# Chunk scores of an RWKV-7 scan as four 64x64 products, their masks for two heads at a time

## The chip, the cores and the metric

The kernel runs on one core of one Trainium2 chip. The metric is the device time of one launch in microseconds, the median of three runs. The engines are TensorE (PE; its weight loads are a row of their own, PEld), VectorE (DVE), ScalarE (ACT), GpSimd (POOL) and SyncE (SP, which starts most DMAs).

## What is computed

The reference is one inference step of a four-layer backbone: layers 0 and 3 are long convolutions, layer 1 is latent attention, and layer 2 is a bidirectional RWKV-7 mixer over 1024 latent and 128 context tokens with 16 heads of 64 channels. Only the recurrence of layer 2 is touched:

```python
def step(S, inp):
    r_t, w_t, k_t, v_t, a_t, b_t = inp
    sa = jnp.einsum('bdhij,bdhj->bdhi', S, a_t)
    S = S * w_t[..., None, :] + sa[..., None] * b_t[..., None, :] + v_t[..., None] * k_t[..., None, :]
    return S, jnp.einsum('bdhij,bdhj->bdhi', S, r_t)

s_fin, y = lax.scan(step, s0.astype(f32), seq)
```

It runs over the tokens in two directions (`d`), for each of the 16 heads.

## The kernel before

The layers run one after another. In layer 2 (`rwkv`) dense projections come first, then `rows_of` writes rows scaled by their decays to DRAM, and then the scan works on chunks of 64 tokens. Two heads lie on the two halves of the 128 partitions (`half`, 64 each). A **segment** is four chunks (or two, for the context) of each direction for one pair of heads; 8 pairs with 5 segments each make 40 segments, 32 of them with four chunks per direction (`n = 4`) and 8 with two.

A segment goes through these jobs:

- `seg_load` fetches its rows from DRAM into `BK` (128 partitions: both heads' channels; per chunk 64 columns of corrections `an` and 64 of keys) and `CT` (for head `e` its own 64 partitions, per chunk 128 columns). The tiles of both are named bg or bk in the trace. `seg_values` fetches values and initial states (`SV`).
- `seg_prep` (the function of the change) makes the scores of a chunk: `BK` of a chunk turned, times `CT` of it, 128 by 128 with the head's 64 channels as contraction (L2015). The upper 64 rows of the result are the scores of the corrections, masked into `NA` (L2017, columns 0 to 63) and `NB` (L2018, columns 64 to 127); the lower 64 rows are the scores of the keys, masked into the half of `CT` that the other head's partitions leave empty (L2019). This is done for each direction and head in a step of its own, so there are four steps, each with one PSUM bank, `n` products and three VectorE operations. POOL then takes the identity from `NA` (L2021), and ACT and POOL split it in an upper and a lower fp16 part (L2023, L2024).
- `seg_inverse` inverts the chunk systems in some 20 short steps (L2055 to L2113), with transposes of `BK` among them (L2099).
- `seg_chain` runs from chunk to chunk: L2136 and L2145 (128 rows, 64 columns per head), L2149 to L2151, L2159, and L2172 (64 rows, 64 columns per head, both heads by turns into one tile `py`), with ACT and DVE operations between them (L2141, L2142, L2153, L2154, L2167).
- `pair_out` finishes a pair of heads (L1939 on).

`stages(w)` sets side by side: the end of chain w, the first half of chain w+1, parts of the inverses w+2, w+3 and w+4, and `seg_prep` of segment w+5. `weave` takes their steps by turns, by the expected number of steps (4 for `seg_prep`, 2n for either chain, 7 for each part of an inverse, 3 for outputs). That is the order in which the code is written; from it the framework's planner lays down the order of each engine's queue ahead of the run, with the code's order as priority, and may let a later instruction go first. Six PSUM banks serve scores, transposes, inverses and chains in turn:

```python
self.set_banks(sc_tp_iv_ch=(0, 1, 2, 3, 4, 5), py0=(6,), py1=(7,))
```

`psum(tag)` hands out the next bank of the turn in the order of the code, and whoever gets it next waits until all that use the tile before are done.

Of the kernel before, what the change touches and what calls it, by code (L numbers as in the profile page):

```python
# [132 lines left out]
def rwkv_constants():  # L133
# [19 lines left out]
    # of each level's mask the columns that change, for four chunks of each direction  # L153
# [11 lines left out]
def weave(*jobs):  # L165
    """Run generators side by side; a job is a generator or (generator, expected number of steps)."""
    for _ in woven(*jobs):
        pass
# [15 lines left out]
def pipelined(gens):  # L184
    """One step advances every generator in flight, the oldest first, and admits the next one."""
    gens, live = list(gens), []
    while gens or live:
        live += gens[:1]
        gens = gens[1:]
        for g in list(live):  # L190
            try:
                next(g)
            except StopIteration:
                live.remove(g)
        yield
# [7 lines left out]
def part_gen(gen, steps):  # L203
    """The next few steps of a generator."""
    for _ in range(steps):
        try:
            next(gen)
        except StopIteration:
            return
        yield  # L210
# [12 lines left out]
class Prog:  # L223
# [22 lines left out]
    def set_banks(self, **kinds):  # L246
        """Which PSUM banks each kind of product (or several kinds together) takes, in turn."""
# [22 lines left out]
    def load_split(self, hi, lo, src, lo_eng=None, pool=None):  # L270
        """DRAM [1024, n <= 128] -> split [128, KC, n], through a staging tile, in two halves."""
# [18 lines left out]
    def mod_part(self, i, part):  # L290
        """Columns (part * 512 ...) of silu(cond) @ mod_w[i] + mod_b[i], for both conditions."""
# [40 lines left out]
    def mod_fast(self, i):  # L332
        """Shift and scale of both conditions on the tensor engine; 16 steps."""
# [30 lines left out]
    def fold_mod(self, i):  # L364
        """h = xn * G + B with xn the normalised rows (or x itself before the first layer)."""
# [21 lines left out]
    def next_group(self, i):  # L387
        """Room for another group of tokens of layer i's input; the RWKV layer takes it unsplit."""
# [6 lines left out]
    def emit_h(self, i, t, xn, pool):  # L395
        """Token tile t of xn (token-major) -> modulated, channel-major, split in hh / hl (or in h32)."""
# [26 lines left out]
    def first_h(self):  # L423
        """The first layer's input; two groups of its rows are turned while the modulation is worked out.

        16 + 6 steps, then 4, 4 and 3 for the groups."""
# [42 lines left out]
    def load_w(self, src):  # L469
        """src [1024, 128]: split weights, k-chunks along the free axis."""  # L470
        nc = self.nc
        wh = self.wp.tile([P, KC, P], F32R, tag="wh", name="wh")
        wl = self.wp.tile([P, KC, P], F32R, tag="wl", name="wl")
        self.load_split(wh, wl, src)
        return wh, wl

    def dense_jobs(self, jobs):
        """Three steps for each (weights [1024, 128], evac(g, psum), then()); weights come one job ahead.

        The first two jobs leave the last group of tokens, which is there last, to the end."""  # L480
# [16 lines left out]
    def boundary(self, i, w_out, y_src, last):  # L497
        """x <- LN(alpha x + gate * (y @ w_out)); y_src(t) loads token tile t as [128, KC, 128], split."""
# [3 lines left out]
        with tc.tile_pool(name="bd", bufs=1, reuse_waits="tile") as pool:  # L502
# [23 lines left out]
            def load_x(t):  # L526
                """alpha x, kept as that after the first layer."""
# [66 lines left out]
    def wout_half(self, w_out, half, turns=True):  # L594
        """Half the columns of w_out, split, in a pool at the far end of the memory; four steps."""
# [11 lines left out]
    def norm_stats(self, s, pool):  # L607
        """Mean and 1 / deviation of every row, in columns 0 and 2."""
# [12 lines left out]
    def load_cst(self, r, k, pool, bufs, raw=False):  # L621
        """DFT constants, split; from the given ones the first time."""
# [14 lines left out]
    def fw_mats(self, r, t):  # L637
        """(re->re, im->re, re->im, im->im) as (hi, lo) pairs."""
# [3 lines left out]
    def stage1_odd(self, xo, out, pool, w):  # L642
        """Odd outputs of the 16-point DFT of eight values; out(r, part)."""
# [4 lines left out]
        # real  # L648
# [14 lines left out]
        # imaginary  # L663
# [16 lines left out]
    def stage1_even(self, xe, out, pool, w):  # L680
        """Even outputs of the 16-point DFT of eight values."""
# [31 lines left out]
    def stage1_inv(self, u, out, pool, w):  # L713
        """u(r, part) -> out(a), a in 0..7 (the inverse of the residues)."""
# [87 lines left out]
    def sine(self, ps, w, freq, fb, y, k):  # L802
        """sin(freq * ps + fb) with the argument reduced to [-pi, pi]."""
# [12 lines left out]
    def features(self, j, pool, fd):  # L816
        """Hidden features of the implicit filter at all positions, split, one block for each pair of taps."""
# [42 lines left out]
    def filters(self, j, pool):  # L860
        """Spectra of the two-sided filter (plus the skip at lag 0), unit by unit -> DRAM."""
# [14 lines left out]
        def weights(q):  # L876
            """Output weights of the filter network, decays and skip of unit q."""
# [91 lines left out]
    def hyena(self, i, j, lead, rest):  # L969
        """lead: steps that come before the first product with h; rest: steps to be done by the end."""  # L970
# [12 lines left out]
        def conv3(col, dst, then):  # L983
            """Job: three-tap convolution of u column tile `col` into dst() [128, W] (a spare column at LS)."""
# [46 lines left out]
        def jobs_gate(b):  # L1031
            """conv3(x0) * silu(z) -> DRAM."""
# [29 lines left out]
        def blocks(q, pool):  # L1062
            """Time blocks of v * x1, token-major."""
# [133 lines left out]
    def mla(self, i, rest):  # L1197
        """rest: steps to be done by the end."""
# [42 lines left out]
        def latents():  # L1241
            """Queries' and keys' compressed forms, token-major -> normalised, channel-major, split."""
# [61 lines left out]
        def early():  # L1304
            """What needs no room of the layer's input."""
# [25 lines left out]
        def pair_values(p):  # L1331
            """Values of a pair of heads, token-major: [v_hi | v_lo] of each head side by side."""
# [29 lines left out]
        def turn(u):  # L1362
            """Positional parts of the queries of four heads, 32 rows each."""
# [28 lines left out]
        def head_prep(h):  # L1392
            """Keys and queries of a head."""
# [35 lines left out]
        def maxima(h):  # L1429
            """The maximum of every query's scores."""  # L1430
# [40 lines left out]
        def attend():  # L1471
            """All heads' softmax and weighted values, 42 steps each."""
# [39 lines left out]
        def finish(h, q0, nq, pv, sm, sz, oT, ri):  # L1512
            """1 / sum, per query in rows, then along the columns; gate."""
# [55 lines left out]
    def rwkv(self, i, rest):  # L1569
        """rest: steps to be done by the end."""  # L1570
# [4 lines left out]
        # r, v, k; scaled rows by chunks: (kk, r) and (minus key correction, key); v by tokens  # L1575
# [11 lines left out]
        # halves of the key gain and of the biases of the decay and of a, for sigmoid(x) = tanh(x / 2) / 2 + 1 / 2  # L1587
# [10 lines left out]
        def head_rsqrt(squares, scale, bias, pool):  # L1598
            """1 / sqrt(scale * (sum of squares over a head's channels) + bias), per group of tokens in PSUM."""
# [20 lines left out]
        # projections  # L1620
# [19 lines left out]
        def mix_ahead(used):  # L1640
            """Mixes as many groups as there is room for, those up to `used` being done with."""
# [6 lines left out]
        def mix(n):  # L1648
            """Group n % 3 of an interpolated input, split: h + mu * (mean of the neighbours - h)."""
# [21 lines left out]
        def differences():  # L1671
            """Mean of the neighbours less h, to DRAM."""
# [9 lines left out]
        def neighbours(s, h, g, ks):  # L1682
            """Sum of the neighbours of h, chunks ks of group g."""
# [12 lines left out]
        def dense(jobs):  # L1696
            """Three steps for each (weights, number of the mix, evac(g, psum)); mixes ahead of their use.

            What evac returns, if anything, is called after the next group's products."""
# [19 lines left out]
        def lora(mi, name, fn):  # L1719
            """First stage of both directions, as a job with its result: upper and lower parts of each, stacked."""  # L1720
# [19 lines left out]
        def lora2(w2, hid, g, n):  # L1740
            """Second stage for a block of channels, a group of tokens and a direction."""
# [60 lines left out]
        def rows_of(b):  # L1802
            """Rows of a head pair, scaled by their decays from either end of their chunk."""
# [5 lines left out]
            for g in range(NG):  # L1809
# [6 lines left out]
                # sums W of the decays' exponents: before each token and before the end of its chunk; backward  # L1816
                # of what is left of the chunk
# [34 lines left out]
                # of the decays: up to and with a token, and before it  # L1852
# [38 lines left out]
        # scan  # L1891
# [37 lines left out]
        def strided(x, first, second, n, m):  # L1929
            """Every other run of m columns of chunks [P, 2 n, 64], from column `first`, resp. in the second half."""  # L1930
# [4 lines left out]
        # (chunks, forward offset, backward offset, number, of)  # L1935
# [3 lines left out]
        def pair_out(b):  # L1939
            """Group norm, bonus, gate."""  # L1940
# [26 lines left out]
        def chunks(x, h, n, of, ob):  # L1967
            """Of rows x [partitions][2 directions][NCH chunks of 128]: n chunks of either direction."""
# [3 lines left out]
        def seg_load(w):  # L1972
            """Scaled rows of a segment."""
# [8 lines left out]
        def seg_values(w):  # L1982
            """Values and initial states."""
# [15 lines left out]
        def seg_prep(sg, w, st):  # L1999
            """Scores of a segment."""  # L2000
# [6 lines left out]
            # scores  # L2007
            NB = nbs[w % 6]
            for d in range(2):
                js = slice(d * n, d * n + n)  # L2010
                mk = mask[:, d:d + 1].broadcast_to([P, n, P])
                for e, h in enumerate(half):
                    ps = bank("sc", P)
                    for c in range(n):
                        nc.tensor.matmul(ps[:, c], BK[h, d * n + c], CT[h, e, d * n + c], start=True, stop=True)  # L2015
# [318 lines left out]
```

## Time and profile before

| | us |
|---|---|
| median of 3 runs | 4655.26 |
| lowest, highest run | 4641.78, 4658.3 |
| span of the profiled execution, first to last instruction | 4633.9 |

The profile is of one execution. Its span leaves out what lies before the first and after the last instruction: the lowest run is 7.9 us above the span, the median 21.4 us. A busy time adds up the times in which an engine has an instruction in flight; matmuls are pipelined, so that a new one starts long before the time given for the one before has passed.

### The profile page before, as it was taken

The numbers are of one execution on the slowest core, as the hardware profiler recorded it, in microseconds if no ns is written. First come the engines' busy times: TensorE is split into PE (matmuls) and PEld (weight loads), VectorE is DVE, ScalarE is ACT, GpSimd is POOL, SyncE is SP. The second block draws the span as 40 slices with busy tenths as digits, with TensorE's granted clock in tenths as the row PEclk, the third lists the DMA queues.
The fourth block names the chain that finished last, engine by engine and source line by source line (L and its number), as shares of the span: only waits on it lengthen the run. The fifth ranks groups of instructions, "written<-read, shape, count | busy, mean of one in ns | idle before, by whom it ended". The sixth has DMA issues, their size and how long they took to land. (4 is left out here: it accounts for less than half of the span.)

```text
span 4633.9 us, 81733 instructions
## 1 busy us (share of the span) xinstructions
PE 4125.1 (89%) x29736; PEld 3562.3 (77%) x29736; DVE 3545.7 (77%) x6307; ACT 2395.0 (52%) x5468; POOL 2358.6 (51%) x1902
## 2 busy tenths in 40 slices
PE   7988988989999998978989777999999889988998
PEld 4888888778777776767877566888888678978986
DVE  6777887655999999587578996777777568967877
ACT  5654433554676676344455544666566456643331
POOL 3655766343787787355546652233333233476550
PEclk8999999988999999989978886999899899989999
DMA  5755455543000001436635462222222423764445
GB/s 174 241 181 174 156 158 171 185 135 98 18 17 24 26 15 39 137 130 196 176 116 184 163 228 74 59 79 71 77 72 65 136 95 113 222 202 151 144 151 181
DMA packets 490975, 582.90 MB, mean 126 GB/s; under 512 B 59819, under 2 KB 378333, under 8 KB 489933
## 3 DMA queue, kind: packets, MB, share of 16 engines
q1 hardware_dynamic: 489068, 576.70, 39.7%
q8 instruction: 235, 3.85, 0.3%
q14 instruction: 168, 1.37, 0.1%
q10 hardware_dynamic: 1504, 0.98, 0.1%
HBM read 413.74 MB, written 161.37 MB: 124 GB/s over the span
## 5 line engine op out<-in xcount | busy, mean ns | idle before, releaser
L262 PE MATMUL ps_mm<-hh,wh 128*128 128x384 f32 x1728 | 594.3, 345 | 47.6 <-ACT hh L267 24.0
L263 PE MATMUL ps_mm<-hl,wh 128*128 128x384 f32 x1728 | 592.8, 343 | 2.6 <-DVE hl L268 1.6
L264 PE MATMUL ps_mm<-hh,wl 128*128 128x384 f32 x1728 | 591.8, 343 | 0.0
L1499 POOL TENSOR_TENSOR sm<-sm,pf 128x512 f32<-128x512 f32 x288 | 443.1, 1539 | 115.4 <-DVE wl L1497 37.3
L268 POOL TENSOR_TENSOR wl<-wraw,wh 128x512 fp32r<-128x512 f32 x212 | 331.2, 1580 | 182.5 <-ACT wh L267 170.1
L262 PEld LDWEIGHTS ps_mm<-hh,wh 128*128 128x128 f32 x1728 | 334.0, 194 | 56.2 <-ACT hh L267 25.1
L1497 DVE TENSOR_TENSOR wl<-pf,wh 128x512 fp32r<-128x512 f32 x288 | 352.1, 1232 | 7.9 <-ACT wh L1493 7.6
L263 PEld LDWEIGHTS ps_mm<-hl,wh 128*128 128x128 f32 x1728 | 333.9, 193 | 7.6 <-DVE hl L268 4.3
L264 PEld LDWEIGHTS ps_mm<-hh,wl 128*128 128x128 f32 x1728 | 333.8, 193 | 3.3 <-issue 3.3
L2139 POOL TENSOR_TENSOR tot<-SV,wcs 64x128 f32<-64x128 f32 x288 | 114.7, 405 | 391.6 <-DVE SV L2167 360.6
L305 POOL TENSOR_TENSOR macc<-macc,mprod 128x512 f32<-128x512 f32 x140 | 212.3, 1517 | 172.3 <-ACT mprod L304 139.6
L263 PE MATMUL ps_mm<-mx,wh 128*128 128x384 f32 x680 | 254.6, 375 | 35.1 <-DVE mx L1669 34.0
L262 PE MATMUL ps_mm<-mx,wh 128*128 128x384 f32 x680 | 257.3, 380 | 13.9 <-ACT mx L1668 5.7
L262 PE MATMUL ps_mm<-woh,hh 128*128 128x512 f32 x576 | 235.8, 411 | 33.8 <-ACT hh L267 31.0
L264 PE MATMUL ps_mm<-mx,wl 128*128 128x384 f32 x680 | 249.3, 368 | 3.7 <-POOL wl L268 3.7
L1492 ACT ACTIVATE pf<-ps_st 128x512 f32<-128x512 f32 x288 | 172.4, 599 | 143.4 <-POOL sm L1499 57.5
L264 PE MATMUL ps_mm<-woh,hl 128*128 128x512 f32 x576 | 234.5, 407 | 2.9 <-DVE hl L268 2.8
L263 PE MATMUL ps_mm<-wol,hh 128*128 128x512 f32 x576 | 232.2, 403 | 0.1
L1437 DVE TENSOR_REDUCE mx<-ps_pj 128x1 f32<-128x512 f32 (+2 forms) x400 | 220.0, 574 | 13.4 <-PE ps_pj L1436 12.6
L302 DVE SCALAR_TENSOR_TENSOR macc<-modw,cond,macc 128x512 f32<-128x512 f32 x140 | 156.4, 1118 | 92.8 <-DMA modw<-mod_w 92.1
L304 ACT ACTIVATE mprod<-modw,cond 128x512 f32<-128x512 f32 x140 | 101.3, 724 | 197.3 <-POOL macc L305 109.3
L1493 ACT ACTIVATE wh<-ps_st 128x512 fp32r<-128x512 f32 x336 | 194.3, 578 | 0.0
(560 smaller groups left out, 13314.6 us busy)
## 6 DMA issues: line engine op xcount, KB each, us to landing
cst<-cst SPq DMA_DIRECT2D x175, 384.0 KB
modw<-mod_w SPq DMA_DIRECT2D x160, 256.0 KB
wraw<-hy_w_in SPq DMA_DIRECT2D x128, 256.0 KB
kd<-kt SPq DMA_DIRECT2D x72, 384.0 KB
kt<-kd SPq DMA_DIRECT2D x72, 384.0 KB
cst<-cst SPq DMA_DIRECT2D x41, 512.0 KB
ctd<-ct SPq DMA_DIRECT2D x24, 768.0 KB
bkd<-bk SPq DMA_DIRECT2D x24, 768.0 KB
```

The costliest lines, as they stand in the source:

```text
L262: mm(ps, lh, rh, start=start, stop=False)
L263: mm(ps, lh, rl, start=False, stop=False)
L264: mm(ps, ll, rh, start=False, stop=stop)
L268: (lo_eng or self.nc.gpsimd).tensor_tensor(lo, src, hi, ALU.subtract)
L302: nc.vector.scalar_tensor_tensor(acc[0], w, s, acc[0], op0=ALU.mult, op1=ALU.add)
L305: nc.gpsimd.tensor_tensor(acc[1], acc[1], wp, ALU.add)
L1437: nc.vector.tensor_reduce(mx[:, t, j:j + 1], ps, AX.X, ALU.max)
L1492: nc.scalar.activation(pf, s, AF.Exp, scale=scale)
L1493: nc.scalar.activation(ph, s, AF.Exp, scale=scale)
L1497: nc.vector.tensor_tensor(pl, pf, ph, ALU.subtract)
L1499: nc.gpsimd.tensor_tensor(sm, sm, pf, ALU.add)
L2139: g_.tensor_tensor(tot[h], SV[e][h, jsl], wc[h].unsqueeze(2).broadcast_to([64, 2, 64]), M)
```

## The change

The two halves of a score product, corrections and keys, become two products with 64 columns of `BK` each, and go into two banks: `ups` takes the scores of the corrections of both heads, each head on its own 64 partitions, and `lows` those of the keys, each head on the other head's partitions. The four products of a chunk (two heads, two halves) then stand on the four quarters of the PE array (row half = the head's channels, column half = the output's partitions). `NA` and `NB` of both heads are masked in one 128-partition operation each; the operations into `CT` stay one per head, and are in the step behind. A segment still has four steps and takes four banks. The rest of the diff only removes comments.

```diff
@@ seg_prep
             for d in range(2):
                 js = slice(d * n, d * n + n)
                 mk = mask[:, d:d + 1].broadcast_to([P, n, P])
+                ups, lows = bank("sc", P), bank("sc", P)
+                for c in range(n):
+                    for e, h in enumerate(half):
+                        other = half[1 - e]
+                        for dst, x in ((ups[h, c], half[0]), (lows[other, c], half[1])):
+                            nc.tensor.matmul(dst, BK[h, d * n + c, x], CT[h, e, d * n + c], start=True, stop=True)
+                v_.tensor_tensor(NA[:, js], ups[:, :n, 0:64], mk[:, :, 0:64], M)
+                v_.tensor_tensor(NB[:, js], ups[:, :n, 64:], mk[:, :, 64:], M)
+                yield
                 for e, h in enumerate(half):
-                    ps = bank("sc", P)
-                    for c in range(n):
-                        nc.tensor.matmul(ps[:, c], BK[h, d * n + c], CT[h, e, d * n + c], start=True, stop=True)
-                    ups, lows = half
-                    v_.tensor_tensor(NA[h, js], ps[ups, :n, 0:64], mk[ups, :, 0:64], M)
-                    v_.tensor_tensor(NB[h, js], ps[ups, :n, 64:], mk[ups, :, 64:], M)
-                    v_.tensor_tensor(CT[half[1 - e], e, js], ps[lows, :n], mk[lows], M)
-                    yield
+                    other = half[1 - e]
+                    v_.tensor_tensor(CT[other, e, js], lows[other, :n], mk[other], M)
+                yield
```

## Rows read from the trace of the kernel before

**Rows 1.** The page: busy time, share of the span and instructions of each engine.
```profile
PE 4125.1 (89%) x29736; PEld 3562.3 (77%) x29736; DVE 3545.7 (77%) x6307; ACT 2395.0 (52%) x5468; POOL 2358.6 (51%) x1902
```

**Rows 2.** Instructions of L2015: count, duration min/median/max ns, first to last start.
```profile
L2015 PE MATMUL ps_sc<-bg,bg x896: 272/272/580, 2855.4 to 3583.4; 64*128 64x128 f32 x180
...
L2015 PE MATMUL ps_sc<-bg x256: 272/272/580, 2761.8 to 3474.1; 64*128 64x128 f32 x128
```

**Rows 3.** By stretch: length, PE, PEld, DVE, ACT, POOL busy (instructions), granted clock, DMA, GB/s.
```profile
2860.00:3640.00 780.00, 756.49 (x11875) 631.35 (x11875) 574.85 (x1581) 481.57 (x1646) 245.84 (x423) 0.92 0.25 71
...
3222.00:3259.00 37.00, 36.73 (x367) 30.18 (x367) 21.22 (x57) 11.96 (x47) 8.93 (x19) 0.50 0.13 33
```

**Rows 4.** Chain that ended last, shares by line: 2860 to 3640, then 2755 to 2860.
```profile
by line: PE ps_sc L2015 16.5%; PE ps_py L2172 9.6%; PE ps_ch L2159 6.8%; PE ps_iv L2086 5.0%; PE ps_py L2145 4.8%; PE ps_tp L2099 4.7%; PE ps_ch L2136 4.2%; PE ps_iv L2080 3.6%; PE ps_iv L2055 3.5%; issue 3.0%; PE ps_iv L2074 2.8%; DVE bg L
...
by line: PE ps_sc L2015 19.1%; DMA bg<-bkd 7.2%; DMA rvk<-rvk 4.9%; issue 4.0%; DVE bk L1864 4.0%; DMA bvd<-row 3.6%; DMA wraw<-rw_w_out 3.5%; PE ps_iv L2055 3.3%; DVE bg L2019 3.1%; PE ps_tp L2099 2.8%; PE ps_iv L2086 2.6%; ACT bd L2023 2.
```

**Rows 5.** The same chain in order of time: start us, us, what.
```profile
3101.50 1.08 PE ps_sc L2015 x8
...
3216.52 3.55 DMA bg<-bkd
...
3224.26 2.00 PE ps_sc L2015 x8
```

**Rows 6.** PE in order of time, a score group cut in two: start us, us, what.
```profile
3161.14 0.48 PE L2015 MATMUL ps_sc<-bg,bg 64*128 64x128 f32 x2
3161.56 0.66 PE L2099 MATMUL ps_tp<-ident,bg 128*128 128x128 f32 x4
3162.14 0.93 PE L2015 MATMUL ps_sc<-bg,bg 64*128 64x128 f32 x6
3163.01 0.34 PE L2136 MATMUL ps_ch<-SV,bg 128*64 128x64 f32 x4
```

**Rows 7.** PE in order of time, at 3102 to 3105; rows with x2 at 3103.99, 3104.82: 0.02 us.
```profile
3102.51 0.33 PE L2172 MATMUL ps_py<-nb,SV 64*64 64x64 f32 x2
3102.77 0.36 PE L2080 MATMUL ps_iv<-hm,bd 128*128 128x32 f16 x8
3103.07 0.44 PE L2086 MATMUL ps_iv<-bd,hm 128*64 128x64 f16 x8
...
3103.99 0.56 PE L2172 MATMUL ps_py<-nb,SV 64*64 64x64 f32 x12
3104.49 0.41 PE L2055 MATMUL ps_iv<-cI,bd 128*128 128x64 f16 x8
3104.82 0.45 PE L2159 MATMUL ps_ch<-SV,bk 128*64 128x64 f32 x8
3105.20 0.33 PE L2172 MATMUL ps_py<-nb,SV 64*64 64x64 f32 x2
...
3103.99 0.27 PE L2172 MATMUL ps_py<-nb,SV 64*64 64x64 f32 x2
...
3104.82 0.28 PE L2159 MATMUL ps_ch<-SV,bk 128*64 128x64 f32 x2
```

**Rows 8.** DVE's groups by shape, 2860 to 3640: busy us, mean ns, idle before and releaser.
```profile
L2019 DVE TENSOR_TENSOR bg<-ps_sc,mask 64x512 f32<-64x512 f32 x116 | 80.5, 694 | 1.7
...
L2017 DVE TENSOR_TENSOR NA<-ps_sc,mask 64x256 f32<-64x256 f32 x116 | 48.3, 416 | 55.5 <-PE ps_sc L2015 53.0 <-POOL tot L2139 0.7 <-issue 0.7
L2018 DVE TENSOR_TENSOR nb<-ps_sc,mask 64x256 f32<-64x256 f32 x116 | 47.1, 406 | 0.0
...
L2178 DVE TENSOR_TENSOR y<-ps_py,y 128x256 f32<-128x256 f32 x28 | 10.5, 417 | 0.1
...
L2017 DVE TENSOR_TENSOR NA<-ps_sc,mask 64x128 f32<-64x128 f32 x24 | 6.8, 283 | 3.3 <-PE ps_sc L2015 2.7
```

**Rows 9.** The score tile's readers, 3075 to 3222: count.
```profile
L2019 DVE TENSOR_TENSOR bg<-ps_sc,mask x29: 426/694/695, 3076.8 to 3216.9; 64x512 f32<-64x512 f32 x21, 64x256 f32<-64x256 f32 x8
```

**Rows 10.** PE's largest wait for L2019, 2860 to 3640: us in total, times, longest.
```profile
PEld ps_tp L2099 <- DVE bg L2019: 2.2, 6, 0.5
```

## The prediction

> **What bounds the kernel now.** I read first the page's busy shares [rows 1]: TensorE (PE) is busy 89% of the span, VectorE (DVE) 77%. That is an average over stages, so only the stage that the edit touches can price it. That stage is the scan; the edited line L2015 runs from 2762 to 3583 us [rows 2]. There the view of busy time by stretch shows PE busy 756 of 780 us, DVE 575, ScalarE (ACT) 482, GpSimd (POOL) 246 and DMA at a quarter [rows 3]. A busy share alone says little of a pipelined engine, so the third view is the chain of work that ended last: in the same 780 us the single largest line is the edited one, PE L2015 with 16.5%, and the lines behind it are PE's too; in the 105 us of filling before it, L2015 has 19.1% beside several DMA waits [rows 4]. So in the scan the end is set by how fast PE gets through its queue, and L2015 is its dearest item. DVE is the next engine, not the present one: it stands idle for 53 us in front of the 256-wide NA operation alone, waiting for L2015 [rows 8].
>
> **What a group of scores costs.** 576 matmul calls (32 segments of 16, 8 of 8) left 1152 instructions [rows 2]: each fp32 call is two. A group of one direction and one head (four chunks, 8 instructions) takes 1.08 us on the chain at granted clock 1.00 and 2.00 us at 0.50 [rows 5]. At the full clock a group cut in two by the planner took 0.42 us for 2 instructions and 0.87 us for 6, each up to the next work's start [rows 6]. The difference is 0.45/4 = 0.112 us per instruction; the rest, 0.42 - 0.22 = 0.19 us, is paid once per group (its first weight load, and the change to another array shape). Check: 8 x 0.112 + 0.19 = 1.09.
>
> **What the edit does to PE.** Each 64x128 product becomes two 64x64 products with the same 128 columns streaming, so a direction of four chunks has 16 calls, 32 instructions, instead of 16. Streaming is what costs, so run one after another they would take 32 x 0.112 + 0.19 = 3.77 us, against 2 x 1.085 = 2.17 us now. Everything hangs on how many run at once. The calls go round four quarters (row half x column half), so there are three prices for a direction: none together 3.77, two together 16 x 0.112 + 0.19 = 1.98, four together 8 x 0.112 + 0.19 = 1.09.
> - Quarters that differ in rows and columns: L2172 has that form (64*64, both heads by turns). Two of its instructions fit into the 0.27 us of one, where two on a single quarter need 0.33; and 12 of them take 0.50 us up to the next start, 0.042 each, whereas a quarter alone pays 0.112/2 = 0.056 for 64 columns plus the 0.15 to 0.19 of a group, 0.82 us or more in all [rows 7]. So two run together.
> - Quarters that share rows: L2159 (128*64) has both heads on the same rows and other columns, two in the 0.28 us of one, 8 in 0.38 us up to the next start [rows 7]. Together as well.
> - Quarters that share columns and write the same output partitions, in two PSUM banks: no row shows it. Its bounds are the prices above, 1.09 and 1.98. I take 1.09, since rows and columns each work and a form that has both halves of either is nearest to them.
> - Order: the calls come quarter by quarter, each as two instructions. If PE started them strictly in that order, the second instruction of one quarter would hold back the first of the next, and the price would be near 1.98. The L2172 rows speak against it: calls of two instructions stand there too, head after head, and the second start within the first 0.02 us is not of the same quarter, since that pair takes 0.33 and not 0.27 [rows 7].
> - Issue: 32 instructions in 8 x 0.112 us is one per 0.028 us; L2080 runs 8 in 0.30 us up to the next start with about 0.1 us of start in it, 0.025 each [rows 7]. It just fits.
>
> [...]
>
> **The sum for PE.** With four together a direction costs what one head costs now: half of L2015 goes. Warm that would be 64 directions x 1.085 + 16 two-chunk directions x (4 x 0.112 + 0.19 = 0.64) = 69 + 10 = 80 us. But only what lies on the chain counts: 16.5% of 780 = 129 us and 19.1% of 105 = 20 us [rows 4], together 149; half is **74 us**. (Some groups there run at 2.00 us, some are covered; the two nearly cancel.)
>
> **VectorE.** NA and NB of both heads become one operation each: per direction one of 0.416 and one of 0.406 us fall away with four chunks, two of about 0.283 with two chunks [rows 8]. 128 partitions cost what 64 cost: 128x256 at L2178 takes 0.417, 64x256 at L2017 0.416 [rows 8]. 64 x 0.822 + 16 x 0.566 = 61.7 us of DVE go. I cost it at nothing, because PE covers DVE (756 against 575 busy); if DVE set the pace instead, it would be at most those 62 us, in place of and not on top of PE's. The two CT corrections (0.694 us each) stay two. POOL's subtraction L2021 waits for NA and may start a step earlier; it is off the chain.
>
> **The wait that is added.** NA now waits for both heads' products instead of one's; at 1.09 us for both that is the wait of now. Behind it on DVE queue the chains' X, SV and hm operations, for which PE waits in turn. More serious are the banks. Before, a bank was freed 1.09 + 0.416 + 0.406 + 0.694 = 2.6 us after its first product. Now `lows` is freed by the CT operations, which are written one step later: 1.09 + 0.82 + 2 x 0.694 = 3.3 us at best. Six banks serve scores, transposes, inverses and chains in a fixed turn. By the code a four-chunk segment takes 4 + 20 + 12 + about 2 (pair_out) = 38 banks; at full clock 29 L2019 operations (7.25 segments) take 147 us [rows 9], 20.3 us a segment, about 18 after the change; a bank comes round after 6/38 x 18 = 2.9 us. So one job wants the bank 0.4 us before it is free. Lower bound nothing, since the planner lets other work pass (it slid L2099 into a score group [rows 6]), upper bound 64 x 0.4 = 26 us with DVE prompt. PE's largest wait for L2019 is 2.2 us over the whole scan [rows 10]; near that row I take 4 us, somewhat more than one such wait.
>
> **Sum.** 74 - 4 = 70 us. Against the profiled execution: span 4633.9 - 70 = 4564. The median of the three runs stands 21.4 us above that span (the lowest 7.9), so the predicted time is 4655.3 - 70 = **4585 us**, 1.5% less. A measurement of this kernel can tell about 0.5%, 23 us, from no change, so "same" is 4632 to 4678. For the likeliest case alone I expect 4560 to 4612: from all 80 plus a few us of DVE on the chain, to the 26 us of bank waits and some idle time.
>
> **Rivals.**
> 1. *Two quarters at a time* (shared columns, shared banks or strict order hold the others back). For it: no row shows four quarters at once. Gain 0.19 x 64 + (1.28 - 8 x 0.112 - 0.19 = 0.19) x 16 = 15 us, so 4640. The change would then not do what it says. Chance 12%. [...]
> 2. *The bank `lows` becomes the bound; slower.* Place: PE stands at the job whose turn is that bank until DVE has done the CT operations. Those are written a quarter of a segment later, 4.5 us; if the planner keeps them there, the hold is 3.3 + 4.5 = 7.8 us against a turn of 2.9, 4.9 too long. PE has up to five jobs side by side to fill that. The gain is 1.1 us per direction, so the sign turns where PE stays idle over 1.1 us per `lows`; at 2 us it costs 64 x 2 = 128 against 74, net 54 slower, 4709. Against it: PE hardly waits for L2019 now, and DVE has a quarter of its time free. Chance 9%.
> 3. *The clock gives it back.* [...] One fall came after PE had stood for 3.55 us at a DMA of bg (3216.52), and then 37 us passed at 0.50 [rows 3, 5]. With a faster PE such stops could show more often. Half-clock time costs about half of itself; twice as much of it costs 62 us: 4647. Chance 8%. The opposite, the falls vanish, gives 62 us more: 4523. Chance 5%; a group of scores at 0.50 would then be rare.
>
> **How the numbers follow.** Forecast 66%, two at a time 12%, bank 9%, clock worse 8%, clock better 5%. Faster: 66 + 5 = 71%; same: 12 + 8 = 20%; slower 9%. The range runs from 4550 (some of the better clock, all 80 us and some DVE) to 4650 (rivals 1 and 3) and leaves out the bank and the fully better clock, 14%.
>
> **What would show it.** In the profile after: a run of 32 score instructions of 64*64 about 1.1 us long on PE (1.98 says rival 1, 3.8 says none together); the share of the score line on the chain about halved; PE still over 93% busy in the scan; the scan about 70 us shorter with DVE's busy time about 62 us less. PE idle or weight loads waiting for the CT operation by tens of us would show rival 2; a granted clock below 0.88 in the scan rival 3. I am wrong from the ground up if PE's queue was not what set the pace: then L2015 is halved and the scan stays as long, with DVE, ACT or DMA ending PE's waits.

## The result, and the profile after

The changed kernel takes 4585.9 us in the median of four runs (4579.6 to 4591.9), the kernel before 4656.8, also in four: a ratio of 0.9855, interval 0.9833 to 0.9877. That is 71 us less, and 1 us from the forecast. The profiled execution has a span of 4588.4 us and took 4590.2; in every run that has both, the time is 1.8 us above the span. So the span of before, 4633.9, belongs to an execution of about 4636 us, one of the shortest, and the 21 us between it and the median are mostly not time outside the span. That execution had also reached the scan some 12 us earlier than the changed kernel's, in code that the change leaves alone. So of the two profiles only the scan is compared.

Busy time by stretch of the changed kernel, columns as in [rows 3]: the scan from 2860 us, where the stretch is 50 us shorter, then the scan with its filling, and last the same for the kernel before (57 us longer).

```profile
2860.00:3590.00 730.00, 698.12 (x12857) 585.08 (x12853) 520.16 (x1425) 477.08 (x1647) 245.27 (x419) 0.97 0.27 75
...
2774.00:3614.00 840.00, 770.10 (x13797) 641.06 (x13792) 589.35 (x1584) 514.18 (x1771) 283.36 (x472) 0.94 0.28 80
...
2762.00:3659.00 897.00, 836.80 (x12644) 694.02 (x12644) 644.90 (x1744) 518.22 (x1771) 281.87 (x472) 0.88 0.26 75
```

PE is still busy 96% of the scan, DVE lost 55 us (520 against 575), and one figure moved that I had not counted on: the granted clock, 0.92 in [rows 3] and 0.97 here. The clock records of both traces hold two values alone, 0.50 and 1.00 (86 records of each in the kernel before, 84 in the changed one), so a mean of 0.92 over 780 us is 780 x 2 x 0.08 = 125 us at the lower level; 0.97 over 730 is 44 us. This **half-clock time** is worked out so from here on (the last digit of the clock leaves some 8 us open).

The chain that ended last, shares by line from 2860 to 3590 us, and some of its pieces in order of time (start, length):

```profile
by line: PE ps_sc L2018 15.7%; PE ps_py L2177 7.6%; PE ps_ch L2141 6.1%; PE ps_py L2150 5.5%; PE ps_ch L2164 5.3%; PE ps_iv L2091 4.4%; PE ps_tp L2104 3.8%; PE ps_iv L2079 3.7%; PE ps_iv L2085 3.6%; issue 3.3%; PE ps_iv L2060 3.3%; ACT bd L
...
3077.26 1.02 PE ps_sc L2018 x16
3078.90 1.04 PE ps_sc L2018 x16
3085.39 1.09 PE ps_sc L2018 x16
3087.14 1.02 PE ps_sc L2018 x16
...
3139.10 1.52 PE ps_sc L2018 x32
```

The score line (L2018 now) had 16.5% of 780 = 129 us on the chain [rows 4]; it has 15.7% of 730 = 115 us. I had forecast half. The pieces say why: there are hardly any runs of 32 instructions, and the six that there are take 1.52 us, not 1.1. The planner laid most of them down as runs of 16, those of one bank, and 16 take 1.02 to 1.09 us. Two such runs a direction are 2.04 to 2.18, against 2 x 1.085 before: two quarters at a time. A stretch of PE and DVE in order of time shows where they part:

```profile
3084.93 0.41 DVE L2081 TENSOR_TENSOR hm<-ps_iv,lms 128x256 f16<-128x256 f32 x1
...
3085.39 1.09 PE L2018 MATMUL ps_sc<-bg,bg 64*64 64x128 f32 x16 [1.29 <-DVE hm L2081]
...
3086.42 0.37 PE L2079 MATMUL ps_iv<-qt,bd 128*128 128x32 f16 x8
3086.53 1.39 DVE L2024 TENSOR_TENSOR bg<-ps_sc,mask 64x512 f32<-64x512 f32 x2 [0.20 <-PE ps_sc L2018]
...
3087.07 1.09 PE L2018 MATMUL ps_sc<-bg,bg 64*64 64x128 f32 x16
...
3088.82 0.42 DVE L2019 TENSOR_TENSOR NA<-ps_sc,mask 128x256 f32<-128x256 f32 x1
```

The first run is that of the keys (its readers are the CT masks, L2024), and it had waited 1.29 us for hm, the mask of an inverse, which is no operand of it. The one thing that the two share is the common turn of banks, so what it waited for was most likely the PSUM bank that hm read. The second run, after another job's eight products, is that of the corrections.

Once in this profile the planner did leave nearly all products of a direction in the order of the code, and that run shows that PE can do what was forecast. PE in order of time; the next work starts at 3218.28:

```profile
3217.26 1.09 PE L2018 MATMUL ps_sc<-bg,bg 64*64 64x128 f32 x28
3218.28 0.28 PE L2091 MATMUL ps_iv<-bd,hm 128*64 128x64 f16 x3
```

28 instructions took 1.02 us up to the next start. By the prices worked out from [rows 6], an estimate, 7 on each quarter at 0.112 us are 0.78, and with the 0.19 that a group costs once 0.97.

VectorE's groups by shape, from 2860 to 3590 us (busy, mean ns, idle before):

```profile
L2024 DVE TENSOR_TENSOR bg<-ps_sc,mask 64x512 f32<-64x512 f32 x114 | 78.4, 688 | 15.9 <-PE ps_sc L2018 14.2
L2019 DVE TENSOR_TENSOR NA<-ps_sc,mask 128x256 f32<-128x256 f32 x57 | 24.2, 424 | 13.7 <-PE ps_sc L2018 12.4
L2020 DVE TENSOR_TENSOR nb<-ps_sc,mask 128x256 f32<-128x256 f32 x58 | 24.0, 415 | 0.0
```

The merged masks cost 424 and 415 ns on 128 partitions, against 416 and 406 on 64 [rows 8], so half of their time went, as worked out. The wait of the NA masks for PE fell from 53 to 12 us, but the CT masks, which had stood idle for 1.7 us in all [rows 8], now wait 14.

So three explanations stand beside each other: the products (129 to 115 us on the chain), VectorE (55 us less busy time in the scan), the clock (125 to 44 us at the lower level). The expectations of the runs below also speak of half-clock time in the scan *with* its filling; in that sense it is 897 x 2 x 0.12 = 215 us before and 101 us after.

### The profile page after: what moved, and what is told of

Same layout as the page of the kernel before. It is cut to its first block, busy times and chain, and to the rows that moved or that the text cites. A ratio compares the mean times of both kernels' runs of the same rounds, so it can differ in the third digit from the quotient of the medians.

```text
span 4588.4 us, 83899 instructions
## 1 busy us (share of the span) xinstructions
PE 4061.0 (89%) x30888; PEld 3510.6 (77%) x30888; DVE 3504.3 (76%) x6147; ACT 2392.5 (52%) x5468; POOL 2360.3 (51%) x1902
```

## Experiments

Each ratio is to runs of the kernel before taken beside it on the same chip, with its 95% interval. Runs 2 and 4 to 8 edit the changed kernel, runs 3, 11 and 12 the kernel before.

### 1. The kernel before, once more

No edit.

> The kernel before, once more, for a second profile of its scan. What is asked: does the half-clock time in the scan come back? In the first profile 125 us of the scan after 2860 us passed at granted clock 0.50, in the changed kernel 44 us. If the clock is the source of the gain, this execution again has 100 us or more of it (mean clock of the whole run 0.91 to 0.92, scan of 890 to 905 us). If the clock of the first profile was an accident of one execution, the half-clock time is under 70 us here while the time stays at 4640 to 4665. Median by all theories: no change, within 0.3%.

Measured: 4647.2 us against 4651.0, ratio 0.998 (0.996 to 1.000). The scan, by stretch:

```profile
2875.00:3655.00 780.00, 755.60 (x11890) 631.62 (x11892) 576.49 (x1582) 481.62 (x1650) 246.69 (x424) 0.92 0.24 71
```

The clock comes out as 0.92 again, 125 us at the lower level. So it was no accident of one execution.

### 2. Quarter products, masks per head

```diff
-                v_.tensor_tensor(NA[:, js], ups[:, :n, 0:64], mk[:, :, 0:64], M)
-                v_.tensor_tensor(NB[:, js], ups[:, :n, 64:], mk[:, :, 64:], M)
+                for h in half:
+                    v_.tensor_tensor(NA[h, js], ups[h, :n, 0:64], mk[h, :, 0:64], M)
+                    v_.tensor_tensor(NB[h, js], ups[h, :n, 64:], mk[h, :, 64:], M)
```

> The changed kernel with its quarter products, but NA and NB masked per head again, four operations of 64 partitions where the change has two of 128: only the VectorE part is undone. If the products on PE bring the gain (the prediction), nothing is lost: 4586, within 10. If the 62 us of VectorE time bring it, all is lost: about 4655. If it is the clock: between, and the half-clock time in the scan goes with the time, about 0.5 us of time for each us of it.

Measured: 4606.4 us, ratio 0.9896 (0.9855 to 0.9936). The scan:

```profile
2860.00:3605.00 745.00, 706.16 (x12861) 592.49 (x12861) 564.69 (x1571) 479.95 (x1645) 246.69 (x422) 0.98 0.26 74
```

Some 45 us of the gain are there without the merged masks, and so is the better clock: 30 us at the lower level. The masks bring the rest, 17 to 20 us (by the ratios and by 4606 to 4586; the two were measured at different times, and the intervals of their ratios overlap). That is neither nothing nor all.

### 3. The kernel before with less VectorE work

```diff
+        for x in nbs:
+            v_.memset(x, 0.0)
...
-                    v_.tensor_tensor(NB[h, js], ps[ups, :n, 64:], mk[ups, :, 64:], M)
```

> The kernel before with its products as they are, but without the masks into NB (160 VectorE operations, about 62 us of VectorE time, the same amount as the change saves); NB is zero throughout, so the contribution of the scores to y inside a chunk is left out, and nothing else. If VectorE's time is the source of the gain: 4586, as the changed kernel. If the products on PE are: 4655, within 10.

Measured: 4638.4 us, ratio 0.9973 (0.9955 to 0.9990): 13 us less (5 to 21). By the operations' times it is what the change saves; VectorE's busy time in the scan with its filling falls by 43 us here (645 to 602) and by 55 in the changed kernel. It is worth 13 us in the kernel before and 17 to 20 in the changed one. It is not the source of the 71, but it was not worth nothing, as I had put it.

### 4. Four quarters together

The order of the products is held: each is queued behind the one written before it, and the one into `lows` is written first.

```diff
+                ins = None
...
-                        for dst, x in ((ups[h, c], half[0]), (lows[other, c], half[1])):
-                            nc.tensor.matmul(dst, BK[h, d * n + c, x], CT[h, e, d * n + c], start=True, stop=True)
+                        for dst, x in ((lows[other, c], half[1]), (ups[h, c], half[0])):
+                            with (tc.issue_after(ins.ins) if ins else ExitStack()):
+                                ins = nc.tensor.matmul(dst, BK[h, d * n + c, x], CT[h, e, d * n + c], start=True, stop=True)
```

> The changed kernel with the order of its score products held: each product is queued behind the one written before it, the one into the second bank first, so that all 16 of a direction stand in one run and the four quarters by turns. In the changed kernel's profile most runs are of 16 instructions into one bank and take 1.02 us, 2.04 a direction, so two quarters at a time. If the hardware can run four together, the runs of 32 here take 1.1 us or less; if not, 1.9 to 2.0. If PE's product time sets the scan, the time falls by a further 64 x 0.95 = 60 us to about 4525. If it doesn't (VectorE or the clock do), it stays within 15 of 4586. If waiting for both banks costs more than it saves, it is over 4600.

Measured: 4560.2 us, ratio 0.9795 (0.9760 to 0.9830), between the 4525 of products that set the scan and the 4586 of products that don't. The scan by stretch, then the chain, shares from 2860 to 3560 us and pieces (this kernel's L2020 is the score line):

```profile
2860.00:3560.00 700.00, 655.21 (x12710) 542.58 (x12705) 509.25 (x1419) 471.61 (x1633) 245.74 (x419) 0.98 0.27 78
...
by line: PE ps_sc L2020 9.1%; issue 5.7%; PE ps_py L2179 5.6%; PE ps_ch L2143 5.4%; PE ps_ch L2166 4.6%; PE ps_py L2152 4.4%; PE ps_iv L2093 4.0%; PE ps_tp L2106 3.7%; ACT bd L2098 3.2%; DVE bg L2026 3.1%; PE ps_iv L2087 3.1%; ACT bd L2047 
...
3093.97 1.03 PE ps_sc L2020 x30
3104.51 0.98 PE ps_sc L2020 x32
3114.19 1.03 PE ps_sc L2020 x30
```

A run of 32 takes 0.98 to 1.03 us, so four quarters do run at once, the two that share columns among them, and the score line has 9.1% of 700 = 64 us on the chain: the half of 129 that I had forecast for the change. But of the 115 - 64 = 51 us only a part arrives in the time (26 us here, 10 in run 10). PE is busy 655 of 700 us now, 94%, and "issue", ACT and DVE lines have moved up the chain: with products that short, PE stands idle for 45 of 700 us where it was 32 of 730.

### 5. The order held, but head after head

The edit against run 4:

```diff
-                for c in range(n):
-                    for e, h in enumerate(half):
+                for e, h in enumerate(half):
+                    for c in range(n):
```

> As the run with four together: the same products, banks, masks and held order, but the order goes head after head, so that only the two quarters of one row half stand side by side. The same number of instructions and streamed columns; only what runs at once differs. If two quarters that share their rows run together and four don't, a run of 32 takes 1.9 to 2.0 us (1.03 with four). PE's product time then is 0.95 us a direction longer, 64 x 0.95 + 16 x 0.45 = 68 us in all. If PE's queue sets the pace, 40 to 68 us of it come back: 4600 to 4628. If the products are hidden: 4560, within 10. If the half-clock time (97 us in the scan there) hangs on four together, it rises towards the 200 us of the kernel before; if on the doubled streaming alone, it stays near 100.

Measured: 4589.9 us, ratio 0.9879 (0.9847 to 0.9911). Pieces of its chain:

```profile
3137.81 1.48 PE ps_sc L2020 x32
...
3271.54 1.52 PE ps_sc L2020 x32
```

A run takes 1.48 to 1.52 us, not the 1.98 that I had worked out for two quarters at a time, so by that estimate the two heads' products run side by side for a part of it. It is 0.49 us more a direction than in run 4 (1.52 against 1.03), 64 x 0.49 = 31 us, with the same instructions, banks and masks (runs of 14 and 16 took 0.60 to 0.77 us in this chain, where 16 of a two-chunk direction, four together, were worked out as 0.64). The time is 30 us longer than in run 4 (0.0084 of the ratio, 39 us), short of the 40 to 68 that I expected. But the clock moved as well. The scan with its filling in run 4, then here:

```profile
2770.00:3581.00 811.00, 731.14 (x13792) 601.78 (x13783) 579.40 (x1580) 513.03 (x1770) 283.83 (x472) 0.94 0.29 82
...
2780.00:3628.00 848.00, 773.26 (x13792) 641.62 (x13790) 580.36 (x1582) 514.15 (x1771) 283.53 (x472) 0.92 0.27 79
```

The half-clock time went from 97 to 136 us, neither staying near 100 nor rising to 200, and half of the difference is 19 us. So of the 37 us between the two scans some 18 to 31 are product time. That much does reach the end of the kernel, as the first part of the prediction has it.

### 6. Keys' masks in the step of the products

```diff
-                yield
                 for e, h in enumerate(half):
                     other = half[1 - e]
                     v_.tensor_tensor(CT[other, e, js], lows[other, :n], mk[other], M)
                 yield
+                yield
```

> The changed kernel with the two masks into CT in the step of the products instead of the step behind, so that the bank of the keys' scores is let go as early as the one of the corrections; everything else is kept. If the wait for this bank costs (the rival of the prediction), the time falls by 10 to 30, to 4556 to 4576. If the planner hides it, 4586 within 8. If it is this bank that keeps the products of the two banks apart in the changed kernel (runs of 16), there are more runs of 32 here.

Measured: 4591.4 us, ratio 0.9877 (0.9844 to 0.9911), the same as the changed kernel; the runs are still mostly of 16 (83, against 86). The bank `lows`, held a step longer, costs nothing that can be measured, and it is not what parts the runs.

### 7. Two banks for scores alone

```diff
-        self.set_banks(sc_tp_iv_ch=(0, 1, 2, 3, 4, 5), py0=(6,), py1=(7,))
+        self.set_banks(sc=(4, 5), tp_iv_ch=(0, 1, 2, 3), py0=(6,), py1=(7,))
```

> The changed kernel with two banks for scores alone and four in turn for the rest (six for all before). Both score banks then come free long before the next direction. If the products of the two banks stand apart because their banks come free at different times in the common turn, they now stand together: runs of 32 at 1.03 to 1.5 us in place of two of 16 at 1.02. Four banks for 34 tiles of a segment come round after 4/34 of about 18 us = 2.1 us instead of 2.9, so inverses and chains wait more. If the bank turn matters most, it is slower: 4600 to 4640; if product time does, faster: 4555 to 4575.

Measured: 4697.0 us, ratio 1.0104 (1.0079 to 1.0128), 111 us slower than the changed kernel. The scan:

```profile
2860.00:3680.00 820.00, 747.04 (x12681) 604.00 (x12677) 512.35 (x1404) 474.65 (x1623) 239.06 (x412) 0.87 0.23 66
```

With four banks in turn for the inverses and chains PE falls to 91% busy, and the clock to 0.87. The miss was on the slow side beyond the range that I gave. So taking two of six banks from the inverses and chains costs much more than it gives, and it is paid twice: PE is idle for 73 us instead of 32, and 213 us pass at the lower level instead of 44. On what parts the score runs it gives a hint: counted in the traces, 720 of the 2304 score instructions stand in runs of 24 or more here, against 304 in the changed kernel. So the common turn of banks has a part in it, and not the whole.

### 8. Runs 4 and 6 in one

The edit against run 4:

```diff
-                yield
                 for e, h in enumerate(half):
                     other = half[1 - e]
                     v_.tensor_tensor(CT[other, e, js], lows[other, :n], mk[other], M)
                 yield
+                yield
```

> Four together (held order) and the masks into CT in the step of the products. If both help on their own, they add: 4560 less 10 to 20, 4540 to 4550. If the bank of the keys' scores costs nothing, 4560 within 8.

Measured: 4570.2 us, ratio 0.9838 (0.9810 to 0.9867). That is 10 us above run 4, with intervals that overlap: no help on top of it, as run 6 said.

### 9 and 10. The changed kernel and the one with four together, side by side

No edits to the two.

> The changed kernel once more, beside the one with four quarters together, in the same rounds. By all theories 0.983 to 0.988 of the kernel before. What is asked is the half-clock time of its scan in a second execution: 100 us, within 20, if the quarter products keep the clock up; anything up to 200 if the first profile was an accident.

> The kernel with four quarters together once more. If PE's queue sets the pace, its shorter products (91 us of PE's queue after 2850 us in place of 129) show in full: 25 to 40 us below the changed kernel of the same rounds, ratio to the kernel before 0.978 to 0.981. If the first comparison was chance, within 10 us of the changed kernel.

Measured: 4580.1 us, ratio 0.9860 (0.9834 to 0.9886), and 4570.0 us, ratio 0.9842 (0.9816 to 0.9867). The scan of the changed kernel in this second execution, and that with four together:

```profile
2860.00:3590.00 730.00, 696.55 (x12929) 583.77 (x12927) 526.69 (x1442) 479.28 (x1654) 246.02 (x422) 0.98 0.27 76
```

```profile
2860.00:3575.00 715.00, 670.28 (x12974) 555.70 (x12970) 518.32 (x1441) 480.95 (x1663) 250.62 (x428) 0.98 0.27 77
```

The clock of the changed kernel holds: 0.98, 29 us at the lower level. The lead of four together is 10 us here and was 26 in the first comparison, where the two were not measured side by side; here the intervals overlap. So it is ahead in both, by less than the 25 to 40 us that I expected, and how far ahead is open.

### 11 and 12. Products of before over all 128 rows, and the control

Run 11 uses both row halves; the other head's half of CT is zero, so the sums stay. Run 12 has the zeros alone.

```diff
             for e, h in enumerate(half):
+                g_.memset(CT[half[1 - e], e, :n2], 0.0)
                 nc.sync.dma_start(flat(CT[h, e, :n2]), ...)
...
-                        nc.tensor.matmul(ps[:, c], BK[h, d * n + c], CT[h, e, d * n + c], start=True, stop=True)
+                        nc.tensor.matmul(ps[:, c], BK[:, d * n + c], CT[:, e, d * n + c], start=True, stop=True)
```

> The kernel before with its score products over all 128 rows in place of 64: the other head's half of CT is set to zero by POOL ahead of the load (two operations a segment), so the sums are the same. The number, length and order of PE's instructions stay; only that all rows of the array take part. If the half-clock time of the scan hangs on what the products occupy, it falls from about 205 to 100 to 150 us and the time with it by 15 to 40, to 4605 to 4635. If it doesn't, both stay: 195 to 215 us, and 4645 to 4665 with POOL's extra work.

> The control to the run before: the kernel before with POOL's zeros alone, products over 64 rows. It prices the two added POOL operations a segment: 0 to 15 us over the kernel before if POOL is off the path, as its 30% in the scan says; half-clock time about 205 us as before.

Measured: 4600.1 us, ratio 0.9906 (0.9875 to 0.9936), and 4665.0 us, ratio 1.0050 (1.0020 to 1.0080). Scan of run 11, PE in order of time there, and scan of run 12:

```profile
2860.00:3610.00 750.00, 715.77 (x11922) 610.11 (x11924) 577.77 (x1587) 482.75 (x1653) 304.34 (x491) 0.96 0.26 74
...
3102.51 1.05 PE L2016 MATMUL ps_sc<-bg,bg 128*128 128x128 f32 x8
3103.41 0.19 PE L2150 MATMUL ps_ch<-X,bd 128*128 128x64 f16 x1
...
3104.99 1.16 PE L2016 MATMUL ps_sc<-bg,bg 128*128 128x128 f32 x8
3106.08 0.32 PE L2173 MATMUL ps_py<-nb,SV 64*64 64x64 f32 x2
```

```profile
2860.00:3670.00 810.00, 783.93 (x12106) 656.12 (x12103) 584.99 (x1603) 493.66 (x1680) 310.82 (x500) 0.89 0.24 69
```

Run 11 shows that the products move the clock. They are as many as before and stream as long; DVE has its old 577 us; and the time is 65 us below the control, 43 below the kernel before, a little more than I had allowed. Of six groups between 3100 and 3125 us, the four with work of the full shape behind them took 0.90 to 1.00 us up to the next start, the two with another shape behind them 1.08 and 1.09. At best that is 0.90 in place of 1.09, so at most 128 x 0.19 = 24 us in all. The half-clock time falls from 810 x 2 x 0.11 = 178 to 750 x 2 x 0.04 = 60 us, and half of the difference is 59 us. The medians are 65 us apart and the two profiled executions 54, so after the cheaper groups 30 us or more are left for the clock; the table below puts it at 51. Whether the rows that the products take are behind this, or the changes of shape that they spare, the run doesn't tell apart. The control was not as neutral as I expected: POOL's zeros cost 22 us (ratio 0.2 to 0.8% above), with more half-clock time than the kernel before.

## Why the prediction was right, point by point

The time came out 1 us from the forecast; the account behind it didn't. Most of its terms were off, and the errors cancelled: that the number fits so well is luck.

- **PE's queue sets the pace in the scan** (chain, [rows 3, 4]): right in the main. Run 5 has 31 us more product time than run 4, and 18 to 31 of the 37 us by which its scan is longer are that; the rest is clock. Not all of a saving arrives: of the 51 us that four together take off the chain, 10 to 26 do.
- **Four quarters together, 1.09 us a direction**: right for the hardware, where the bounds were 1.09 and 1.98 (run 4: 0.98 to 1.03; the 28 instructions in the changed kernel: 1.02). Wrong for this kernel. The step that failed is "the calls go round four quarters": that is the order of the code, and the planner's order was what counted. I had a row that showed the planner cutting a score group in two [rows 6], and used it only as a comfort for the banks. With runs of 16 the score line lost 14 us on the chain of the scan, not the 64 that were half of it there (74 with the filling). That rival 1 would come by another way (not the hardware, the queue) I hadn't seen; its sign, 1.98 us a direction, is what the profile shows (2.04), yet its time, 4640, is not.
- **VectorE at nothing**: wrong. The amount was right, about 62 us by the operations' times, but "PE covers it" took a share of busy time for a cover. The merge is worth 17 to 20 us in the changed kernel (run 2) and its amount 13 in the kernel before (run 3). DVE stands in the jobs' dependencies, on the chain in stretches; that a shorter operation there lets PE's next product start earlier is my reading, and no run tries it alone.
- **The bank `lows`, 4 us and a slower rival of 9%**: the 4 us are within nothing (run 6). That banks can set the pace was not far-fetched: run 7 takes two from the others and is 111 us slower than the changed kernel.
- **The clock**: the case with 5%, "the falls vanish, 62 us", came true by two thirds: 125 to 44 us at the lower level in the scan (29 in run 9), worth 40 to 48 us at half of the 81 to 96 (the table below, which takes in the filling, gives 43 and 50). I had worked out its price, 62 us, from [rows 3] (0.08 of 780, as a group took 1.08 us at 1.00 and 2.00 at 0.50 [rows 5]), and gave it a small chance for want of a reason why products should touch it. Run 11 shows that they do.

How the gain divides can be estimated from the traces. Take the scan from its first to its last score product, and give each PE instruction the time up to the next one's start, at most its own. Those that started at the lower level are set against the mean of their line at the full clock; what they took beyond it is the price of that level. In us:

| | before | changed | run 2 | run 4 | run 5 | run 12 | run 11 |
|---|---|---|---|---|---|---|---|
| first to last score product | 822 | 757 | 777 | 731 | 768 | 835 | 781 |
| score products, at the full clock | 159 | 141 | 139 | 101 | 131 | 161 | 149 |
| PE's other work, at the full clock | 545 | 534 | 545 | 541 | 542 | 540 | 537 |
| added by the lower level | 64 | 20 | 24 | 16 | 28 | 76 | 25 |
| PE idle | 54 | 62 | 68 | 73 | 68 | 58 | 69 |

So of some 64 us between the two profiled scans about 43 come through the clock (50 between runs 1 and 9), 18 through shorter score products and 11 through PE's other work, and PE stands idle 8 us longer. The quarter products alone (run 2) save 19 us of product time, but PE waits 13 us longer, so nearly all of their 45 us is the clock. Run 4 saves another 40 us of product time, of which longer waits and PE's other work take back 18. In the medians the whole gain is 63 to 71 us, of which the merged masks make 17 to 20.

What parts the runs of the two banks is shown only in part: a score run waits for an inverse's mask, with which it shares nothing but the turn of banks, and in run 7, where the scores have banks of their own, more of them stand together. Run 6 shows that the hold of `lows` isn't the reason; the planner's own grounds were not tried.

Of the five signs that I had named, PE's busy share (96%) and VectorE's time (55 us less for 62) came out as said; the runs of 32, the halved share on the chain and a scan shorter by 70 (57 in the two profiles) did not.

The kernel of run 4 is the fastest of all here: 4560 and 4570 us in its two comparisons, 0.9795 and 0.9842 of the kernel before, though in the second its interval overlaps that of the changed kernel.

## What to carry to other kernels

Where several small products should share the array, look at the order of the engine's queue, not at the order of the code: here a direction took 2.04 us as the planner laid its products down, 1.48 to 1.52 head after head, and 0.98 to 1.03 with the four quarters by turns. Read the queue's runs in the profile, and hold the order if the planner parts them. A sum that meets the measured time proves nothing until each term has its own row after the change. And when a matmul changes its shape, read the granted clock of its stretch before and after, since here more of the gain came through the clock than through the instructions.

## What the runs showed of the hardware

- Four 64x64 fp32 products on the four quarters run at once: 32 instructions of 128 columns take 0.98 to 1.03 us, 0.03 us each (run 4). In these runs two row halves write one bank at different partitions, and two quarters of the same columns write two banks, and a run still takes about half of the 1.98 us worked out for two quarters at a time. As runs of 16, each into one bank on two quarters, 32 take 2.04 us (2 x 1.02, changed kernel).
- The granted clock moved with the products. Between runs 12 and 11 the products are as many, of 128 columns each, and only their rows change: over 64 of the 128 rows 178 us of the scan passed at 0.50, over all rows 60, with PE busy 97% of the scan in the first and 95% in the second. With quarter products it was 29 to 44 us in the changed kernel, in the kernel before 125 (twice). There PE was also busy 36.7 of 37 us at 0.50 [rows 3], behind a stop of 3.55 us at a DMA [rows 5]; whether the stop brought the fall, no run tries.
- A score group over all rows took 0.90 to 1.00 us up to the next start where a product of the same shape came behind it, and 1.08 to 1.09 where one of another shape did (run 11): up to 0.19 us a group for the change of shape. The prediction gives the first weight load a part in the 0.19 us that a group costs once; no run tries that alone.
